# Half of w_down as seven products of block sums, with weight sums on VectorE and some low parts by DMA

## The chip, the cores and the metric

The kernel runs on one core of a Trainium2 chip. The metric is the device time of one execution in microseconds (us). The kernel before takes 1104.13 us, the median of three runs (1103.97 to 1104.59).

## The reference, cut to what matters

One layer of a decoder trunk on 256 positions of 2048 channels, in float32. A mixing part (combined projection, convolution, matrix memory, gating, output projection) is followed by the part that the change rewrites:

```python
hm = rmsnorm(x, ln_mlp_g[l]) @ w_up[l]               # (256, 2048) @ (2048, 8192)
x = x + jnp.square(jax.nn.relu(hm)) @ w_down[l]      # (256, 8192) @ (8192, 2048)
return rmsnorm(x, final_g)
```

## The kernel before, in words

TensorE multiplies in fp32r, a rounded form of float32, so every operand is cut in two: a high part (rounded) and a low part (the rest). A product of two cut operands needs three matmuls: high by high, high by low, low by high.

All weights come as pieces of 128 x 2048 floats (1 MB), loaded by SyncE in the order of use into a ring of 4 buffers (`raw`). A piece is two units of 128 x 1024. For each unit ScalarE casts the high part (`hi`, L131) and VectorE subtracts it from the raw values (`lo`, L132); each has 5 buffers. `advance(h)` is called before the matmuls of unit h: it issues loads up to 6 pieces ahead and cuts units up to 4 ahead. A scheduler sets the order on PE, ACT, DVE and SP, with the cutting of weights raised in priority; GpSimd keeps the program's order.

The MLP goes in four quarters of 2048 hidden channels. In the up half of a quarter, 16 tiles of 128 hidden channels are made, two to a PSUM pair of banks (`up`): each tile takes 16 wide matmuls of 512 columns (high weights by high and low x, L217) and 16 narrow ones of 256 columns (low weights by high x, L222). PSUM holds two such pairs, so that one fills while the other is read out: ScalarE copies one half to `u_sb` (L675), VectorE adds the other half (`u_t`, L677), takes the squared ReLU (L678), and u is cut (L679, L680). In the down half, four column blocks of 512 are made for the two halves of the 256 rows, 16 k tiles each: three matmuls of 512 columns for every k tile and row half (`dn`, L240 to L242). VectorE adds the result times the norm's factor to the residual `xr` (L694). In the last quarter the final norm follows (L698 to L718), with products by `final_g` on GpSimd (L700).

An eighth of the MLP is thus 8 up tiles, and 8 k tiles x 4 column blocks x 2 row halves x 3 = 192 matmuls of w_down.

Of the kernel before, what the change touches and what calls it, by code (L numbers as in the profile page):

```python
# [14 lines left out]
P = 128  # L15
# [8 lines left out]
DFF = 8192  # L24
NQ = 4
EPS = 1e-6
RAW_BUFS = 4
W_BUFS = 5
SPLIT_AHEAD = 4
DMA_AHEAD = 12  # L30
UNITS = 2
TAIL = 4
# [26 lines left out]
def trunk(ctx: ExitStack, tc: tile.TileContext, x, xt, w_t, w_n, w_o, w_u, w_d, gw, gm_w, cols, rows, out):  # L59
    nc = tc.nc  # L60
    const = ctx.enter_context(tc.tile_pool(name="const", bufs=1))
    big = ctx.enter_context(tc.tile_pool(name="big", bufs=1))
    wpool = ctx.enter_context(tc.tile_pool(name="wpool", bufs=W_BUFS))
    work = ctx.enter_context(tc.tile_pool(name="work", bufs=1))
    two = ctx.enter_context(tc.tile_pool(name="two", bufs=2))
    small = ctx.enter_context(tc.tile_pool(name="small", bufs=1))
    acc = ctx.enter_context(tc.tile_pool(name="acc", bufs=2, space=PSUM))
    misc = ctx.enter_context(tc.tile_pool(name="misc", bufs=4, space=PSUM))
# [7 lines left out]
    pieces = [w_n[i] for i in range(8)]  # L76
    pieces += [w_t[i] for i in range(16)]
    pieces += [w_n[i] for i in range(8, 32)]
    pieces += [w_o[i] for i in range(16)]
    for q in range(NQ):  # L80
        pieces += [w_u[q * 16 + i] for i in range(16)]
        pieces += [w_d[q * 16 + i] for i in range(16)]
    raws, his, los = {}, {}, {}
    state = {"dma": 0, "split": 0, "later": {}}
    n_units = len(pieces) * UNITS

    def load_piece():
# [9 lines left out]
        elif j < 4:  # L97
            for i in range(2):
                k = 4 * j + 2 * i
                nc.sync.dma_start(xs4[:, k:k + 2, :], xt3[:, k:k + 2, :])  # L100
                nc.sync.dma_start(raw[:, i * 1024:(i + 1) * 1024], pieces[j][:, i * 1024:(i + 1) * 1024])
        else:
# [11 lines left out]

    def split_unit():

        h = state["split"]
        state["split"] += 1
        parts = 1
        if h < 4 * UNITS:  # L120
            kn = 4 // UNITS
            for k in range(h * kn, (h + 1) * kn):
                x_prep(k)
            parts = 2 if h < P2 else 1
        raw = raws[h // UNITS][:, h % UNITS * UW:(h % UNITS + 1) * UW]
# [49 lines left out]
    cmask = const.tile([P, P], F32, name="cmask")  # L175
# [28 lines left out]
    def mm_t(pt, act, j, order=range(2 * UNITS)):  # L204
# [3 lines left out]
        for n, o in enumerate(order):  # L208
# [581 lines left out]
```

## Time and profile before

| | |
|---|---|
| median of three runs | 1104.13 us |
| the profiled execution's own time | 1103.79 us |
| its span in the profile | 1102.1 us |
| PE busy | 1089.6 us, 99% of the span |
| DVE busy | 689.6 us, 63% |
| ACT busy | 530.7 us, 48% |
| POOL busy | 57.8 us, 5% |
| granted TensorE clock | 0.998 of full speed |
| DMA | 211.05 MB, mean 191 GB/s |

PE's busy time counts matmuls whose modelled durations overlap, so that a busy PE is one that never waits, and the distance from start to start is the cost of a matmul. For DVE and ACT, too, an instruction that follows at once starts some 0.1 us before the end shown for the one ahead. Times in the rows below count from the span's start.

### The profile page before, as it was taken

What the parts mean: (1) busy time and instruction counts of PE and PEld (TensorE: products, weight loads), DVE (VectorE), ACT (ScalarE), POOL (GpSimd) and SP (SyncE); (2) the same over time, 40 slices, a digit from 0 to 9 for tenths busy, and PEclk for the clock granted to TensorE, in tenths of its full rate; (3) what the DMA queues carried; (4) which work ended last, traced back from release to release, by engine and by line L of the source; (5) the groups of instructions that cost most, each with busy time, mean ns of one, the idle gap of its engine ahead of it and who ended that gap; (6) DMA issues with size and microseconds to landing.
All of it is one profiled execution on the core that took longest, in us unless ns stands there. A gap on an engine that the chain in (4) does not pass through costs nothing.

```text
span 1102.1 us, 13677 instructions
## 1 busy us (share of the span) xinstructions
PE 1089.6 (99%) x5447; PEld 924.1 (84%) x5447; DVE 689.6 (63%) x841; ACT 530.7 (48%) x655; POOL 57.8 (5%) x70
## 2 busy tenths in 40 slices
PE   9999999999999999999999999999999999999997
PEld 7888888888888888888888888888888888888885
DVE  7788999665665556555546565555565555565553
ACT  7574755444564454443334443334444334444442
POOL 1002120040300000000000000000000000000111
PEclk9999999999999999999999999999999999999999
DMA  9645445554475555555555555555555555555531
GB/s 347 261 172 179 167 163 190 182 191 169 175 305 186 180 189 186 187 183 194 194 210 184 186 178 193 196 197 202 186 189 180 194 198 205 189 183 177 196 141 76
DMA packets 32176, 211.05 MB, mean 191 GB/s; under 512 B 3697, under 2 KB 4081, under 8 KB 7665
## 3 DMA queue, kind: packets, MB, share of 16 engines
q1 hardware_dynamic: 32112, 210.19, 54.1%
q8 instruction: 42, 0.69, 0.3%
q14 instruction: 22, 0.17, 0.0%
HBM read 208.08 MB, written 2.10 MB: 191 GB/s over the span
## 4 chain that ended last, share of the span: by engine, by line
PE 90%; DVE 5%; issue 3%; POOL 1%; ACT 1%; DMA 0%; SPq 0%; ACTq 0%; POOLq 0%; DVEq 0%
PE up L217 21%; PE up L222 11%; PE dn L242 10%; PE dn L241 10%; PE dn L240 10%; PE wo L240 3%; PE wo L242 3%; PE wo L241 3%; PE qk L217 2%; DVE lo L132 2%; DVE cvo L313 2%; PE o L240 1%; PE o L242 1%; PE o L241 1%; PE v L241 1%
## 5 line engine op out<-in xcount | busy, mean ns | idle before, releaser
L132 DVE TENSOR_TENSOR lo<-raw,hi 128x1024 fp32r<-128x1024 f32 (+1 forms) x388 | 474.6, 1226 | 340.8 <-ACT hi L131 340.6
L131 ACT CAST hi<-raw 128x1024 fp32r<-128x1024 f32 (+1 forms) x388 | 402.8, 1042 | 449.7 <-PE dn L242 188.7
L217 PE MATMUL up<-x,hi 128*128 128x512 f32 x1024 | 245.6, 391 | 0.0
L217 PEld LDWEIGHTS up<-x,hi 128*128 128x128 f32 x1024 | 188.0, 188 | 36.2
L240 PE MATMUL dn<-hi,u 128*128 128x512 f32 x480 | 186.7, 389 | 0.0
L241 PE MATMUL dn<-lo,u 128*128 128x512 f32 x480 | 186.7, 389 | 0.0
L242 PE MATMUL dn<-hi,u 128*128 128x512 f32 x480 | 186.7, 389 | 0.0
L222 PEld LDWEIGHTS up<-x,lo 128*128 128x128 f32 x1024 | 131.4, 191 | 5.1
L222 PE MATMUL up<-x,lo 128*128 128x256 f32 x1024 | 133.0, 283 | 0.0
L241 PEld LDWEIGHTS dn<-lo,u 128*128 128x128 f32 x480 | 90.1, 188 | 18.8
L240 PEld LDWEIGHTS dn<-hi,u 128*128 128x128 f32 x480 | 90.1, 188 | 18.7
L242 PEld LDWEIGHTS dn<-hi,u 128*128 128x128 f32 x480 | 90.1, 188 | 18.7
L217 PE MATMUL qk<-xg,hi 128*128 128x512 f32 x256 | 62.4, 392 | 1.0 <-DVE qk_t L413 1.0
L217 PEld LDWEIGHTS qk<-xg,hi 128*128 128x128 f32 x256 | 46.7, 188 | 10.9 <-PE qk L217 1.8
L313 DVE SCALAR_TENSOR_TENSOR cvo<-aT,colv,cvo 128x256 f32<-128x256 f32 x120 | 53.9, 498 | 0.0
L240 PE MATMUL wo<-hi,mix 128*128 128x512 f32 x128 | 50.4, 394 | 0.0
L241 PE MATMUL wo<-lo,mix 128*128 128x512 f32 x128 | 50.1, 391 | 0.0
L242 PE MATMUL wo<-hi,mix 128*128 128x512 f32 x128 | 49.9, 390 | 0.0
L700 POOL TENSOR_TENSOR xr<-xr,fgv 128x512 f32<-128x512 f32 x6 | 9.5, 1606 | 765.9 <-ACT jf L698 765.9
L679 ACT CAST u<-u_t 128x512 fp32r<-128x512 f32 x32 | 19.9, 621 | 53.0 <-DVE u_t L678 53.0
L680 DVE TENSOR_TENSOR u<-u_t,u 128x512 fp32r<-128x512 f32 x32 | 22.1, 691 | 19.3 <-ACT u L679 19.3
L222 PEld LDWEIGHTS qk<-xg,lo 128*128 128x128 f32 x256 | 32.9, 191 | 1.3
(224 smaller groups left out, 1006.5 us busy)
## 6 DMA issues: line engine op xcount, KB each, us to landing
raw<-in_w_u SPq DMA_DIRECT2D x64, 1024.0 KB, 4.7
raw<-in_w_d SPq DMA_DIRECT2D x64, 1024.0 KB, 4.7
raw<-in_w_n SPq DMA_DIRECT2D x28, 1024.0 KB, 4.7
raw<-in_w_t SPq DMA_DIRECT2D x16, 1024.0 KB, 4.7
raw<-in_w_o SPq DMA_DIRECT2D x16, 1024.0 KB, 4.8
raw<-in_w_n SPq DMA_DIRECT2D x6, 512.0 KB, 7.6
xr<-in_x SPq DMA_DIRECT2D x2, 1024.0 KB, 6.5
out<-xr SPq DMA_DIRECT2D x8, 256.0 KB, 2.6
```

What stands on the lines that cost most here:

```text
L131: nc.scalar.copy(hi[:, s], raw[:, s])
L132: nc.vector.tensor_tensor(out=lo[:, s], in0=raw[:, s], in1=hi[:, s].bitcast(F32), op=ALU.subtract)
L217: nc.tensor.matmul(pt[:, i, :], lhsT=hi[:, kk, :], rhs=act[:, k, :, :], start=(k == 0), stop=(k == NK - 1))
L222: nc.tensor.matmul(pt[:, i, 0:T], lhsT=lo[:, kk, :], rhs=act[:, k, 0, :], start=False, stop=False)
L240: nc.tensor.matmul(pt[t], lhsT=xh, rhs=hi[:, kk, :], start=(k == 0), stop=False)
L241: nc.tensor.matmul(pt[t], lhsT=xh, rhs=lo[:, kk, :], start=False, stop=False)
L242: nc.tensor.matmul(pt[t], lhsT=xl, rhs=hi[:, kk, :], start=False, stop=(k == NK - 1))
L313: nc.vector.scalar_tensor_tensor(out=o, in0=a, scalar=w, in1=o, op0=ALU.mult, op1=ALU.add)
L679: nc.scalar.copy(u[:, 2 * g:2 * g + 2, 0, :], tt)
L680: nc.vector.tensor_tensor(out=u[:, 2 * g:2 * g + 2, 1, :], in0=tt, in1=u[:, 2 * g:2 * g + 2, 0, :].bitcast(F32), op=ALU.subtract)
L700: nc.gpsimd.tensor_tensor(out=xr[:, t, cs], in0=xr[:, t, cs], in1=fgv[:, cs], op=ALU.mult)
```

## The change

Seven of the eight stages of 1024 hidden channels form columns 0 to 1023 of the down product by a 2 x 2 x 2 scheme with seven products: the blocks are two row halves, two k tiles and two column blocks of 512. Of the blocks of u (A11, A12, A21, A22) four sums are formed on GpSimd (S1 to S4, `up_out`), of the four blocks of w_down four sums on VectorE (`sum_piece`, tiles `sa` and `sb`); seven products of three matmuls each go to seven PSUM banks (`dn_a`), over four pairs of k tiles. `dn_out` puts them together into `xr`, on VectorE and GpSimd. Columns 1024 to 2047, and all of the last stage, go as before (`mm_n`, tiles `dp` and `dl`).

The up tiles of the next stage are interleaved: between the products of a pair stand two up tiles, each in the eighth bank (tag `up`, one buffer). The squared ReLU is now a square of ReLU(up) times the norm's factor, which is broadcast along the columns once by two small matmuls, so that the residual gets a plain sum.

A pair's weights are one piece with four units (512 or 1024 columns wide, with their own buffers, two of the wide and one of the narrow kind). For six of the eight up tiles of a stage the low part of the second unit is formed by a DMA on GpSimd's queue: ScalarE writes `hi`, which is `raw` rounded, and `lo`, which is minus `raw` rounded (so it costs ScalarE two operations and VectorE none), and the DMA adds `raw` to `lo`, reading the raw buffer. The raw ring has 3 buffers in place of 4, cutting goes 5 units ahead, and sums are taken 2 pieces ahead. In the query and key projections, narrow and wide matmuls alternate (`mm_t`).

```diff
--- before.py
+++ after.py
+NS = 8
+NP = 4
-RAW_BUFS = 4
+RAW_BUFS = 3
 W_BUFS = 5
-SPLIT_AHEAD = 4
-DMA_AHEAD = 12
+SPLIT_AHEAD = 5
+DMA_AHEAD = 6
+SUM_AHEAD = 2
 UNITS = 2
+ADDED = (0, 1, 3, 4, 5, 7)
...
+    for st in range(NS):
+        last = st == NS - 1
+        for g in range(0 if last else NP):
+            jdn[st, g] = stream(w_pair(st, g))
+            four.add(jdn[st, g])
+            for i in range(2):
+                sl = 2 * g + i
+                j = jup[st + 1, sl] = stream(w_u[(st + 1) * 2 * NP + sl])
+                units += [(jdn[st, g], 2 * i), (jdn[st, g], 2 * i + 1), (j, 0), (j, 1)]
+                if sl in ADDED:
+                    added.add((j, 1))
...
+    def sum_piece():
+
+        j = state["sum"]
+        state["sum"] += 1
+        if j not in four:
+            return
+        raw = raws[j]
+        s13 = ph["mlp"].tile([P, 1024], F32, tag="sum", name=f"sa{j}", bufs=2)
+        s24 = ph["mlp"].tile([P, 1024], F32, tag="sum", name=f"sb{j}", bufs=2)
+        nc.vector.tensor_tensor(out=s13.rearrange("p (a n) -> p a n", a=2),
+                                in0=raw[:, 512:1536].rearrange("p (a n) -> p a n", a=2),
+                                in1=raw[:, 0:512].rearrange("p (a n) -> p a n", a=1).broadcast_to([P, 2, 512]),
+                                op=ALU.add)
+        nc.vector.tensor_tensor(out=s24[:, 0:512], in0=s13[:, 512:1024], in1=raw[:, 512:1024], op=ALU.add)
+        nc.vector.tensor_tensor(out=s24[:, 512:1024], in0=s24[:, 0:512], in1=raw[:, 1536:2048], op=ALU.add)
+        sums[j] = (s13, s24)
...
+        pool, tag, bufs = (wpool, "", None) if j not in four else (ph["mlp"], "4", 2) if n == UW else (ph["mlp"], "5", 1)
+        hi = pool.tile([P, n], F32R, tag="hi" + tag, name=f"hi{h}", bufs=bufs)
+        lo = pool.tile([P, n], F32R, tag="lo" + tag, name=f"lo{h}", bufs=bufs)
+        his[h], los[h] = hi, lo
+        if (j, k) in added:
+            nc.scalar.copy(hi, src)
+            nc.scalar.mul(lo, src, -1.0)
+            nc.gpsimd.dma_start(out=lo, in_=src, accum_op=ALU.add)
+            return
...
+            for kk in range(kn):
+                k = o % UNITS * kn + kk
+                a = dict(lhsT=hi[:, kk, :], rhs=act[:, k, :, :])
+                b = dict(lhsT=lo[:, kk, :], rhs=act[:, k, 0, :])
+                if k < NK - 1:
+                    nc.tensor.matmul(pt[:, i, :], start=(k == 0), stop=False, **a)
+                    nc.tensor.matmul(pt[:, i, 0:T], start=False, stop=False, **b)
+                else:
+                    nc.tensor.matmul(pt[:, i, 0:T], start=False, stop=False, **b)
+                    nc.tensor.matmul(pt[:, i, :], start=False, stop=True, **a)
...
+    banks = ctx.enter_context(tc.tile_pool(name="banks", bufs=7, space=PSUM, reuse_waits="tile"))
+
+    def bank(name, tag="dn", bufs=None):
+        return banks.tile([P, 512], F32, tag=tag, name=name, bufs=bufs)
...
+    def up_out(pt, st, sl):
+
+        g, i = divmod(sl, 2)
+        if i == 0:
+            uf[st, g] = mlp.tile([P, 8, P], F32, tag="uf", name=f"uf{st}_{g}", bufs=2)
+        u = uf[st, g]
+        sb = mlp.tile([P, T], F32, tag="usb", name=f"usb{st}_{sl}")
+        nc.scalar.copy(sb, pt[:, T:2 * T])
+        q = mlp.tile([P, T], F32, tag="uq", name=f"uq{st}_{sl}", bufs=2)
+        nc.vector.tensor_tensor(out=q, in0=pt[:, 0:T], in1=sb, op=ALU.add)
+        nc.vector.scalar_tensor_tensor(out=q, in0=q, scalar=0.0, in1=rb, op0=ALU.max, op1=ALU.mult)
+        nc.scalar.activation(u[:, 0:4:3, :] if i == 0 else u[:, 1:3, :], q.rearrange("p (t n) -> p t n", t=2), AF.Square)
+        if i == 1 and st < NS - 1:
+            nc.gpsimd.tensor_tensor(out=u[:, S3:S1 + 1, :], in0=u[:, A21:A21 + 1, :].broadcast_to([P, 2, P]),
+                                    in1=u[:, A11:A22 + 1:2, :], op=ALU.subtract)
+            nc.gpsimd.tensor_tensor(out=u[:, S2, :], in0=u[:, A11, :], in1=u[:, S1, :], op=ALU.subtract)
+            nc.gpsimd.tensor_tensor(out=u[:, S4, :], in0=u[:, A12, :], in1=u[:, S2, :], op=ALU.subtract)
...
+    def split(d, u):
+        nc.scalar.copy(d[:, :, 0, :], u)
+        nc.vector.tensor_tensor(out=d[:, :, 1, :], in0=u, in1=d[:, :, 0, :].bitcast(F32), op=ALU.subtract)
+
+    def split_pair(st, g):
+        u = uf.pop((st, g))
+        ua[st, g] = mlp.tile([P, 4, 2, P], F32R, tag="ua", name=f"ua{st}_{g}", bufs=2 * NP)
+        split(ua[st, g], u[:, 0:4, :])
+        if st < NS - 1:
+            us[st, g] = mlp.tile([P, 4, 2, P], F32R, tag="us", name=f"us{st}_{g}", bufs=NP)
+            split(us[st, g], u[:, 4:8, :])
...
+            ah, al = form(st, g, a)
+            cs = slice(b * 512, (b + 1) * 512)
+            nc.tensor.matmul(acc7[a], lhsT=ah, rhs=hi[:, cs], start=(g == 0), stop=False)
+            nc.tensor.matmul(acc7[a], lhsT=ah, rhs=lo[:, cs], start=False, stop=False)
+            nc.tensor.matmul(acc7[a], lhsT=al, rhs=hi[:, cs], start=False, stop=(g == NP - 1))
...
+        nc.scalar.copy(p1, acc7[A11])
+        dve(x12, x12, acc7[S4], ALU.add)
+        dve(x11, x11, acc7[A12], ALU.add)
+        dve(x12, x12, acc7[S1], ALU.add)
+        dve(x22, x22, acc7[S1], ALU.add)
+        dve(v, p1, acc7[S2], ALU.subtract)
+        dve(w, v, acc7[S3], ALU.subtract)
+        dve(x21, x21, acc7[A22], ALU.add)
+        pool(x11, x11, p1, ALU.add)
+        pool(x12, x12, v, ALU.subtract)
+        pool(x21, x21, w, ALU.add)
+        pool(x22, x22, w, ALU.subtract)
...
+    for st in range(NS - 1):
+        acc7 = {}
+        for g in range(NP):
+            dn_a(st, g, 0, ((A11, 1), (S4, 0)), acc7)
+            dn_a(st, g, 1, ((A12, 0),), acc7)
+            up_tile(st + 1, 2 * g)
+            dn_a(st, g, 2, ((S1, 1), (S3, 0)), acc7)
+            dn_a(st, g, 3, ((S2, 0), (A22, 1)), acc7)
+            if g == NP - 1:
+                dn_out(st, acc7)
+            up_tile(st + 1, 2 * g + 1)
+        for c in (2, 3):
+            pt = [bank(f"dp{st}_{c}{t}") for t in range(2)]
+            mm_n(pt, act_n(st), jpl[st, c], nk=2 * NP)
```

ScalarE around an up tile's end, before. `hi` is a high part, `u_sb` the copy out of PSUM, `u1` the cut of u; the number behind a name tells units and buffers apart, and in brackets stand the engines or queues waited for.

```order
L131 CAST hi226_5278<-raw113_5092 128x1024 [waits DMAHW0_49,PE_49,Activation_49]
L131 CAST hi227_5298<-raw113_5092 128x1024 [waits PE_49,Activation_49]
L131 CAST hi228_5328<-raw114_5142 128x1024 [waits DMAHW1_49,PE_49,Activation_49]
L675 COPY u_sb17_5318<-up17_5233 128x512
L131 CAST hi229_5344<-raw114_5142 128x1024 [waits PE_49,Activation_49]
L679 CAST u1_4588<-u_t17_5320 128x2x256 [waits DVE_49]
```

And now, at the end of the first up tile of a stage (`up3_0`; `sa` is a weight sum, `uf` the values of u, `usb` the copy, and raw109 holds the next-but-two piece of w_up).

```order
L205 CAST hi233_5412<-raw107_5218 128x512 [waits DMAHW3_49,PE_49]
L205 CAST hi234_5424<-raw108_5257 128x1024 [waits DMAHW4_49]
L205 CAST hi235_5439<-raw108_5257 128x1024 [waits PE_49]
L205 CAST hi238_5507<-raw109_5296 128x1024 [waits DMAHW5_49,PE_49]
L785 COPY usb3_0_5406<-up3_0_5356 128x256
L205 CAST hi232_5385<-raw107_5218 128x1024 [waits DMAHW2_49,PE_49]
L205 CAST hi236_5459<-sa107_5359 128x1024 [waits DVE_49,PE_49]
L789 ACTIVATE uf3_0_5405<-uq3_0_5408 128x2x128 [waits DVE_49]
```

In both, a cast stands directly ahead of the copy that frees the tile's bank; now this cast waits for a load (DMAHW5) as well as for PE.

TensorE from one up tile to the next, before: the tile in the other pair of banks follows at once.

```order
L217 MATMUL up15_5049<-x2_2597,hi215_5022 128x512 [waits Activation_49]
L217 MATMUL up15_5049<-x2_2597,hi215_5022 128x512 x7
L217 MATMUL up16_5141<-x2_2597,hi216_5052 128x512 [waits DVE_49]
L217 MATMUL up16_5141<-x2_2597,hi216_5052 128x512 x7
L222 MATMUL up16_5141<-x2_2597,lo216_5053 128x256 x8
```

And now, the last three of the thirteen product matmuls that stand between tiles `up3_0` and `up3_1`, and the whole of `up3_1`.

```order
L832 MATMUL dn2_2_5432<-lo229_5336,ua2_0_4704 128x512
L833 MATMUL dn2_2_5432<-hi229_5336,ua2_0_4704 128x512
L831 MATMUL dn2_0_5340<-hi232_5385,ua2_1_4859 128x512 [waits Activation_49]
L765 MATMUL up3_1_5436<-x2_2607,hi230_5348 128x512 [waits DVE_49]
L765 MATMUL up3_1_5436<-x2_2607,hi230_5348 128x512 x7
L769 MATMUL up3_1_5436<-x2_2607,lo230_5349 128x256 x8
L769 MATMUL up3_1_5436<-x2_2607,lo231_5365 128x256 [waits DMASW5_49]
L769 MATMUL up3_1_5436<-x2_2607,lo231_5365 128x256 x7
L765 MATMUL up3_1_5436<-x2_2607,hi231_5364 128x512 x8
```

The tile's first matmul waits for VectorE's add out of the only `up` bank, and its second low part for a DMA of GpSimd's queue.

GpSimd before: between the mixing part and the last quarter's norm nothing stands in its queue.

```order
L192 TENSOR_TENSOR lnc_2556<-lnr_2554,nhalf_106 128x2 [waits DVE_49]
L608 TENSOR_TENSOR og_2240<-og_2240,numx_791 128x512 [waits Activation_49] x2
L700 TENSOR_TENSOR xr_2594<-xr_2594,fgv_3290 128x512 [waits DMAHW2_49,DMAHW6_49,Activation_49,Pool_49]
L700 TENSOR_TENSOR xr_2594<-xr_2594,fgv_3290 128x512 [waits DMAHW3_49,PE_49,Activation_49]
L700 TENSOR_TENSOR xr_2594<-xr_2594,fgv_3290 128x512 [waits Activation_49]
```

And now, from the putting together of stage 1 to the adding DMAs at the start of stage 2 (`p1`, `v`, `w` are sums of products).

```order
L843 TENSOR_TENSOR xr_2604<-xr_2604,p11_5109 128x512 [waits DVE_49]
L843 TENSOR_TENSOR xr_2604<-xr_2604,v1_5110 128x512 [waits DVE_49]
L843 TENSOR_TENSOR xr_2604<-xr_2604,w1_5111 128x512 [waits DVE_49]
L843 TENSOR_TENSOR xr_2604<-xr_2604,w1_5111 128x512
L791 TENSOR_TENSOR uf2_3_5082<-uf2_3_5082 128x256 [waits Activation_49]
L793 TENSOR_TENSOR uf2_3_5082<-uf2_3_5082 128x128 [waits Pool_49]
L794 TENSOR_TENSOR uf2_3_5082<-uf2_3_5082 128x128 [waits Pool_49]
L200 DMA lo227_5299<-raw105_5125 128x1024 [waits DMASW3_49,DMAHW0_49,DVE_49,PE_49]
L200 DMA lo231_5365<-raw106_5184 128x1024 [waits DMASW0_49,DMAHW1_49,DVE_49,Activation_49]
L791 TENSOR_TENSOR uf3_0_5405<-uf3_0_5405 128x256 [waits Activation_49]
```

The two DMAs stand behind the sums of u of the stage's last pair, and ahead of those of the next.

## Rows read from the trace of the kernel before

**Rows 1.** The page, part 1 and the first line of part 4.

```profile
PE 1089.6 (99%) x5447; PEld 924.1 (84%) x5447; DVE 689.6 (63%) x841; ACT 530.7 (48%) x655; POOL 57.8 (5%) x70
...
PE 90%; DVE 5%; issue 3%; POOL 1%; ACT 1%; DMA 0%; SPq 0%; ACTq 0%; POOLq 0%; DVEq 0%
```

**Rows 2.** The longest waits of PE: who waited for whom, us, times, longest.

```profile
PE warm L163 <- DVE warm L159: 1.1, 1, 1.1
PE qk L217 <- DVE qk_t L413: 1.0, 2, 0.7
```

**Rows 3.** Busy time by stretch, the MLP without its last block.

```profile
core 0: us, PE busy (x) PEld busy (x) DVE busy (x) ACT busy (x) POOL busy (x), PEclk, DMA share, GB/s
...
390.00:1007.00 617.00, 617.00 (x3203) 530.84 (x3203) 350.46 (x348) 270.81 (x294) 0.00 (x0) 1.00 0.55 191
```

**Rows 4.** PE in order of time: start, us, operation; one quarter's down and up halves.

```profile
478.42 0.39 PE L240 MATMUL dn<-hi,u 128*128 128x512 f32 x1
478.64 0.39 PE L241 MATMUL dn<-lo,u 128*128 128x512 f32 x1
...
565.46 0.84 PE L217 MATMUL up<-x,hi 128*128 128x512 f32 x3
...
654.52 0.39 PE L240 MATMUL dn<-hi,u 128*128 128x512 f32 x1
```

**Rows 5.** DVE by line and shape: busy us, mean ns of one, idle before.

```profile
L132 DVE TENSOR_TENSOR lo<-raw,hi 128x1024 fp32r<-128x1024 f32 x380 | 469.4, 1238 | 338.8 <-ACT hi L131 338.7
L680 DVE TENSOR_TENSOR u<-u_t,u 128x512 fp32r<-128x512 f32 x32 | 22.1, 691 | 19.3 <-ACT u L679 19.3
L424 DVE SCALAR_TENSOR_TENSOR qk_c<-qk_z,colv,qk_c 128x256 f32<-128x256 f32 x48 | 20.9, 478 | 5.9 <-ACT qk_c L421 5.7
L355 DVE TENSOR_TENSOR scr<-gps,scr 36x256 f32<-36x256 f32 x1 | 0.4, 409 | 0.0
```

**Rows 6.** ACT by line and shape, columns as in Rows 5.

```profile
L131 ACT CAST hi<-raw 128x1024 fp32r<-128x1024 f32 x380 | 398.2, 1051 | 447.8 <-PE dn L242 188.7 <-PE up L217 135.5 <-PE wo L242 36.6
L473 ACT COPY numx<-num 128x258 f32<-128x258 f32 x8 | 2.7, 375 | 0.5 <-PE num L472 0.5
```

**Rows 7.** ACT and DVE in order of time at an up half's end.

```profile
478.66 1.05 ACT L131 CAST hi<-raw 128x1024 fp32r<-128x1024 f32 x1 [2.69 <-PE up L217]
479.62 0.57 ACT L675 COPY u_sb<-up 128x512 f32<-128x512 f32 x1
...
479.75 1.23 DVE L132 TENSOR_TENSOR lo<-raw,hi 128x1024 fp32r<-128x1024 f32 x1 [2.52 <-ACT hi L131]
480.89 0.68 DVE L677 TENSOR_TENSOR u_t<-up,u_sb 128x512 f32<-128x512 f32 x1
```

**Rows 8.** DVE and POOL in order of time, 1030 to 1036 us.

```profile
1030.02 1.22 DVE L132 TENSOR_TENSOR lo<-raw,hi 128x1024 fp32r<-128x1024 f32 x1
1032.55 2.17 DVE L132 TENSOR_TENSOR lo<-raw,hi 128x1024 fp32r<-128x1024 f32 x1 [1.31 <-ACT hi L131]
...
1030.50 3.14 POOL L700 TENSOR_TENSOR xr<-xr,fgv 128x512 f32<-128x512 f32 x2 [728.75 <-ACT jf L698]
```

**Rows 9.** POOL by line and shape, columns as in Rows 5.

```profile
L571 POOL TENSOR_TENSOR sq<-sq 128x512 f32<-128x512 f32 x1 | 1.3, 1296 | 5.8 <-ACT sq L570 5.8
L554 POOL TENSOR_TENSOR csum<-cvo 128x256 f32<-128x256 f32 x1 | 0.7, 737 | 0.0
```

**Rows 10.** DMA issues: KB each, median us to landing.

```profile
raw<-in_w_u SPq DMA_DIRECT2D x64, 1024.0 KB, 4.7
raw<-in_w_n SPq DMA_DIRECT2D x6, 512.0 KB, 7.6
gng<-in_rows SPq DMA_DIRECT2D x1, 512.0 KB, 4.2
```

**Rows 11.** GB/s in 40 slices of 498 to 520 us (0.55 us each).

```profile
GB/s 432 45 0 0 0 209 89 402 372 447 387 0 0 0 0 134 179 402 447 447 313 15 0 0 0 238 89 343 477 432 328 15 0 0 0 223 209 343 432 447
```

More of the change, by code (lines that the diff above doesn't have):

```diff
@@ L101, in load_piece @@
                 nc.sync.dma_start(raw[:, i * 1024:(i + 1) * 1024], pieces[j][:, i * 1024:(i + 1) * 1024])
+        elif j in four:
+            for i in range(2):
+                nc.sync.dma_start(raw[:, i * 1024:(i + 1) * 1024], pieces[j][i])
         else:
@@ L118, in split_unit @@
         state["split"] += 1
+        j, k = units[h]
         parts = 1
@@ L264, in trunk @@
     pt = acc_tile("cg")
-    mm_n(pt, xg, 0)
+    mm_n(pt, halves(xg), 0)
     for o_ in (0, 4):
@@ new lines, in trunk, with up_units, wide, narrow @@
+    uf, ua, us = {}, {}, {}
+    def up_units(pt, j, k):
+        kn = NK // UNITS
+        h = index[j, k]
+        hi = his.pop(h).rearrange("p (k n) -> p k n", k=kn)
+        lo = los.pop(h).rearrange("p (k n) -> p k n", k=kn)
+        def wide():
+            for kk in range(kn):
+                kt = k * kn + kk
+                nc.tensor.matmul(pt, lhsT=hi[:, kk, :], rhs=x2[:, kt, :, :], start=(kt == 0), stop=(kt == NK - 1))
+        def narrow():
+            for kk in range(kn):
+                nc.tensor.matmul(pt[:, 0:T], lhsT=lo[:, kk, :], rhs=x2[:, k * kn + kk, 0, :], start=False, stop=False)
+        if k == 0:
+            wide()
+            narrow()
+        else:
+            narrow()
+            wide()
@@ new lines, in trunk @@
+    for k in range(UNITS):
+        for sl in range(2):
+            j = jup[0, sl]
+            if k == 0:
+                us["pt", sl] = bank(f"up0_{sl}")
+            advance(index[jup[0, 0], 0] + 2 * k + sl)
+            up_units(us["pt", sl], j, k)
+    rps = bank("rps")
+    for t in range(2):
+        dg = mlp.tile([P, P], F32, tag="usb", name=f"r_dg{t}")
+        nc.vector.tensor_scalar(out=dg, in0=ident, scalar1=r2[:, t:t + 1], scalar2=None, op0=ALU.mult)
+        nc.tensor.matmul(rps[:, t * P:(t + 1) * P], lhsT=ones, rhs=dg, start=True, stop=True)
@@ new lines, in trunk, with norm_part @@
+                nc.vector.tensor_tensor(out=xr[:, t, cs], in0=pt[t], in1=xr[:, t, cs], op=ALU.add)
+    st = NS - 1
+    fgv = keep.tile([P, D], F32, tag="A", name="fgv")
+    nc.sync.dma_start(fgv, rows[0:1, R_FG:R_FG + D].broadcast_to([P, D]))
+    def norm_part(c, t):
+        cs = slice(c * 512, (c + 1) * 512)
+        jk = mlp.tile([P, 512], F32, tag="p1", name=f"jf{c}{t}")
+        nc.scalar.activation(jk, xr[:, t, cs], AF.Square, accum_out=st3[:, t, c:c + 1])
+        if c < 3:
+            nc.gpsimd.tensor_tensor(out=xr[:, t, cs], in0=xr[:, t, cs], in1=fgv[:, cs], op=ALU.mult)
```

278 lines of the change are left out of this document (154 added, 124 removed).

## Prediction

> **What bounds the kernel now.** I read the page's shares first: TensorE is busy for 99% of the span, and 90% of the chain that ended last runs over it [rows 1]. Then its waits: the longest two are 1.1 and 1.0 us [rows 2], so nothing is to be won by taking waits away. By stretches, from 390 to 1007 us TensorE is busy for 617 of 617 us at the full clock, VectorE for 351 (57%), ScalarE for 271 (44%), and the DMA engines are 55% busy [rows 3]. The kernel's time is its number of matmuls times their pitch; the other engines have slack, and the change spends it.
>
> The pitch comes from the starts in order of time [rows 4]: a quarter's down half begins at 478.42, its up half at 565.46, the next down half at 654.52. The first is 384 matmuls of 512 columns: 87.04 / 384 = 0.2267 us each. The second is 16 up tiles: 89.06 / 16 = 5.566 us each. Of VectorE's and ScalarE's operations I take durations [rows 5, 6], and where they follow at once the distance of the starts, about 0.1 less: a low part of 1024 costs 1.14 us (479.75 to 480.89), a cast 0.96 (478.66 to 479.62) [rows 7].
>
> **What is removed.** A stage's w_down takes 192 matmuls now. The half that is rewritten had 96 and gets 7 products x 4 pairs x 3 = 84. That is 12 fewer in each of seven stages, 84 x 0.2267 = **-19.0 us**. A stage is then 8 x 5.566 + (84 + 96) x 0.2267 = 85.3 us long, where it was 88.1. That wide and narrow matmuls alternate in the query and key projections I cost at nothing: the same matmuls stand there, and TensorE goes from one kind to the other within each up tile now without a wait [rows 2, 4]. The norm's tail keeps its operations.
>
> **The single bank for up tiles.** Before, the next tile goes to another pair of banks. Now its first matmul waits until ScalarE's copy and VectorE's add have emptied the only bank; product matmuls fill the time between. The order gives their number ahead of a stage's tiles 1 to 7: 13, 8, 12, 9, 12, 13, 13, or 2.95, 1.81, 2.72, 2.04, 2.72, 2.95 and 2.95 us. Undisturbed, emptying takes: start of the copy 0.24 after the tile's end (478.42 to 478.66 for the first operation of ScalarE [rows 4, 7]), the copy 0.375 by a 258-column one [rows 6], the add 0.41 by a 256-column one [rows 5], together 1.03: hidden everywhere. But casts and low parts have raised priority, and behind tiles 0, 5 and 6 the order puts a cast directly ahead of the copy and a low part ahead of the add. The trace has just this: cast at 478.66, copy 479.62, low part 479.75, add 480.89 [rows 7]. With 0.41 for the add the bank is free at 481.30, 2.88 us after 478.42, against 2.95. That is a tie, and I charge 0.2 us to each of the three. In the windows of 1.81 and 2.04 a low part that has just begun makes 1.03 + 1.14 = 2.17, late by 0.36 or 0.13; not every time, so 0.1 each. Sum 0.8 a stage, x 7 = **+5.6**. Bounds: 0, and one low part's 1.14 at each of the seven tiles, 8.0 a stage, 56 us.
>
> **The adding DMAs and three raw buffers.** No row shows a DMA that adds. From a 512 KB load's 4.2 us at the least to 7.6 at the most, where 1 MB lands in 4.7 [rows 10]: of the 4.7 about 2.4 us are movement (in the slices, four or five of 0.55 us at some 400 GB/s, then a gap [rows 11]), so 2.3 are fixed. A DMA that adds reads two times 512 KB, each 1.2 us of movement: 2.3 + 2.4 = 4.7, my estimate. As lower bound 3.5 (2.3 and one 512 KB movement); upper 7.6.
>
> What waits for it: the tightest place is a stage's start. There the order has the DMA for the second tile's low part (the one with DMASW5) behind ScalarE's multiplication, which comes about 1.7 us ahead of the stage's first product by the order of casts. When it has landed, raw's buffer may be loaded again (4.7 us), and the cast of that load stands directly ahead of the copy that frees the bank of the stage's first tile. So the cast can begin at D - 1.7 + 4.7 = D + 3.0; that tile ends after 9 products and itself, 2.04 + 5.57 = 7.6, and 0.24 later ScalarE would take the cast. Hidden up to D = 4.8. At 4.7 it is a tie again: 0.1 in six stages, **+0.6**. TensorE's own wait for that low part has more: tiles 0 and 1 and the products between lie ahead. A later adding DMA of the same stage stands on GpSimd behind the sums of u; it starts about 14.5 us into the stage and is needed at 21.2, so it is hidden up to D = 6.7.
>
> By the Trainium skill ("DMA: Bandwidth & Descriptors", section "Anatomy of one DMA — SWDGE (gpsimd) path") a DMA of GpSimd's queue takes 2.0 us and its bytes at 436 GB/s. By "Collectives: The Full Stack" of the Trainium skill (section "The bandwidth ceiling: the fold count and why AG ≠ RS ≠ AR") an add needs two source reads and goes at about half the rate. Both together would be 2.0 + 2.4 = 4.4 us, an estimate by which this term falls to 0; no trace here shows such a DMA.
>
> **VectorE.** For each stage of 85.3 us: 30 low parts of 1024 (six of 36 are gone to the DMAs, twelve belong to the pairs) x 1.14 = 34.2; four weight sums of the same width 4.6; 31 operations of 512 (eight sums, four low parts, eight of u, seven of the putting together, four residuals) x 0.60, from 0.69 less 0.1 = 18.6; eight adds and eight ReLU operations of 256, (0.41 + 0.48 - 0.18) x 8 = 5.7 [rows 5, 7]. Sum 63.1, or 74%. On top comes GpSimd: a low part that runs beside one of GpSimd's operations with two inputs takes 2.17 in place of 1.22 us [rows 8]. GpSimd gets, a stage, four times an operation of 256 (0.74) and two of 128 (0.46 each, estimated from 0.74 and 1.30), and four of 512 (1.30) [rows 9], 11.8 us. If VectorE stood for all of that, it has 75 of 85.3 us: tight, and still not the bound.
>
> The Trainium skill ("SBUF — State Buffer", section "Who interferes with whom") says that a VectorE instruction with two SBUF inputs and a GpSimd instruction that reads SBUF exclude each other wholly. By that rule all of the 11.8 us count; the trace agrees, with 2.17 beside 1.22 us, so that the 75 is taken as it stands.
>
> **The rest.** Start of the MLP with three raw buffers, two small matmuls that broadcast the norm's factor, and the hand-overs of banks between products and plain blocks: 1.5 us, **+1.5**, from about one exposed low part (1.14) and one add (0.41); bounds 0 and 6 (a 1 MB load, 4.7, exposed once, and one low part). ScalarE has, a stage, 36 casts and six multiplications of 0.96, and some 12 us of smaller ones: 52 of 85.3, no bound.
>
> **Sum.** -19.0 + 5.6 + 0.6 + 1.5 = -11.3. The profiled execution took 1103.79 us (1102.1 of it span); 1092.5, and the median of the runs lies 0.34 above that one: **1093 us**.
>
> **Rivals.**
> First, everything is hidden: neither bank nor DMA costs anything. For it: free emptying takes 1.03 us against 1.8 to 2.95, and VectorE and ScalarE have slack. Against it: raised priority of casts, as in rows 7. -19.0 + 1.5 = -17.5, **1087 us**. Chance 0.20.
>
> Second, VectorE becomes the bound. 75 us of work lie in a fixed order with waits for ScalarE, for PE and for GpSimd; 338.8 us of its idle time now lie ahead of low parts, behind casts [rows 5], about 0.9 for each. With 2 us of idle time in each of a stage's eight tiles it takes 75 + 16 = 91, 5.7 over, x 7 = 40: 1103.8 - 19.0 + 40 = **1125 us**. It decides from (85.3 - 75) / 8 = 1.3 us of idle time a tile. Against it: low parts are cut five units ahead. Chance 0.10.
>
> Third, and mainly on the slower side, the adding DMA lands late, through the raw buffers. At D = 7.6 the reload holds ScalarE's queue by 7.6 - 4.8 = 2.8 us and the later low part is late by 7.6 - 6.7 = 0.9, in six stages: 22.2. With 5.6 and 1.5: -19.0 + 29.3 = +10.3, **1114 us**. It makes the kernel slower from D = 6.75 on: at 6.7 the 1.9 x 6 = 11.4 us nearly use up the 11.9 that are left of the gain, and beyond it grows by 12 us for each us of D. For it: 512 KB loads of 7.6 us exist; a raw ring of three gives little play. Against it: those pieces are halves of one load that queue behind each other, and the other 512 KB one took 4.2. Chance 0.15.
>
> **How the numbers follow.** The forecast has 0.55; its own range is 1088 to 1099 (bank term between 0.2 and 1.7 a stage). A measurement here tells some 0.2%, 2.2 us, from no change. Faster: the forecast's 0.52, the first rival's 0.20 and a little of the third, 0.73; slower: 0.10 and most of the third, and the forecast's tail, 0.19; same 0.08. The range leaves out the second rival and the outer part of the others: 1085 to 1114.
>
> **What would show it.** TensorE's matmuls of 512 columns at the same 0.227 us pitch, and 84 fewer. In TensorE's waits, a group of up tiles behind VectorE's add, of 0.1 to 0.3 us in about five of eight tiles: the bank term. ScalarE's casts behind raw loads at the stages' starts: the raw term; and low parts of up tiles behind GpSimd's DMA queue, which should hardly be there. Adding DMAs that land in 4 to 5 us. VectorE at 80 to 90% of a stage, with low parts of 2 us beside GpSimd's sums. The prediction is wrong if VectorE stands above 95% in a stage, or if adding DMAs take over 6.5 us, or if TensorE's waits come to under 2 or over 15 us in all.

## The result, and the profile after

The changed kernel takes 1192.85 us (median of four runs, 1187.45 to 1196.28) against 1104.05 of the kernel before: 1.0799 times as long, 95% interval 1.0756 to 1.0842. The prediction was 1093 us, 1085 to 1114, faster with a chance of 0.73. It was wrong on the side as well as in size. Of its own signs of being wrong one showed: TensorE's waits of 68 us, where over 15 was its limit.

First the page after, its shares and the first line of its chain, then TensorE's waits (who waited for whom, us, times, longest); they answer to [rows 1, 2]:

```profile
PE 1111.0 (93%) x5367; PEld 931.5 (78%) x5367; DVE 833.9 (70%) x1086; ACT 649.8 (54%) x884; POOL 210.7 (18%) x225
...
PE 59%; DMA 17%; issue 7%; ACT 7%; POOL 5%; DVE 4%; SPq 0%; POOLq 0%; ACTq 0%; DVEq 0%
```

```profile
PE up L765 <- DVE uq L787: 48.6, 16, 5.4
PE dn L831 <- ACT hi L205: 19.8, 8, 3.9
```

TensorE had two waits of 1 us before; now two groups make up 68.4 us, and DMAs have 17% of the chain that had 0%. By stage (columns as in [rows 3]; seven stages with products, each from its first product on):

```profile
434.00:537.00 103.00, 91.81 (x439) 77.44 (x438) 73.57 (x88) 59.55 (x80) 26.87 (x28) 0.93 0.61 197
537.00:639.00 102.00, 91.45 (x437) 76.56 (x436) 68.94 (x82) 54.16 (x71) 21.22 (x23) 0.93 0.60 195
639.00:742.00 103.00, 91.37 (x439) 76.15 (x438) 69.32 (x83) 54.29 (x72) 21.77 (x23) 0.95 0.60 194
742.00:844.50 102.50, 91.68 (x438) 77.09 (x437) 69.64 (x82) 54.71 (x71) 21.71 (x23) 0.93 0.62 197
844.50:943.80 99.30, 90.24 (x437) 75.80 (x436) 69.08 (x82) 54.40 (x71) 22.37 (x22) 0.95 0.62 200
943.80:1045.00 101.20, 91.26 (x437) 76.51 (x436) 69.12 (x82) 54.29 (x71) 21.50 (x23) 0.95 0.61 198
1045.00:1140.00 95.00, 89.75 (x437) 75.07 (x437) 59.73 (x73) 47.97 (x62) 10.07 (x9) 0.96 0.68 219
```

They take 706 us where the prediction's 85.33 a stage make 597.3: all of the loss is here. What lies ahead and behind takes 1192.7 - 706 = 486.7 us; before, with seven stages of 88.05 taken off, it is 485.7. The 108.7 us divide in two. 68.4 are TensorE's waits. The rest, 40.3 us, is time in which TensorE is busy, 637.6 us of these stages by the rows above where 597.3 would do; and the granted clock accounts for about that much: one minus the shares 0.93 to 0.96, times each stage's length, summed, is 40 us. The clock falls after a wait; three stretches around one of them (same columns):

```profile
676.30:683.87 7.57, 2.18 (x11) 1.49 (x9) 2.81 (x4) 4.67 (x6) 0.00 (x0) 0.98 0.77 300
683.87:687.50 3.63, 3.63 (x11) 2.92 (x12) 3.63 (x5) 1.41 (x3) 2.54 (x3) 0.57 0.01 2
691.00:700.00 9.00, 9.00 (x49) 7.77 (x48) 5.19 (x7) 5.74 (x8) 0.00 (x0) 1.00 0.82 305
```

TensorE is busy for 2.18 of 7.57 us and waits for the rest; then it works without a pause at 0.57, mostly its 1.2 GHz level, for 3.6 us; a few us later it has 2.4 GHz again. A wait of 5.4 us so costs 1.6 us more (3.63 x 0.43), after other waits up to 2.7 (an up tile of 32 matmuls, 5.34 us from its first to its last start, takes 8.09 at 479.83). The prediction had no such term.

Where a wait comes from, the chain shows (start, us, what), in the third of these stages, which begins at 639.17:

```profile
637.12 1.07 ACT lo L199
...
638.48 5.58 DMA lo<-raw
...
644.20 6.45 DMA raw<-in_w_u
...
650.73 0.07 ACT hi L205
...
651.68 0.37 ACT usb L785
652.05 0.95 ACT hi L205
...
653.05 0.79 PE dn L831
653.84 3.19 PE up L765 x8
...
667.47 1.05 ACT lo L199
...
668.83 5.95 DMA lo<-raw
...
675.29 6.84 DMA raw<-in_w_d
...
682.25 1.23 DVE sa L167
683.48 0.35 DVE uq L787
```

ScalarE writes minus raw, the DMA adds raw, only then the same raw buffer is loaded again, only then ScalarE can cast the new piece (650.73). Behind that cast ScalarE's queue has the copy that empties the bank of the stage's first tile (651.68), and behind the copy the cast of a high part (652.05). What TensorE waits for here is this high part, for 3.4 us: a product ahead of the second tile needs it (L831; in six of the seven stages the first long wait is of this kind). The bank was no earlier: VectorE's add ended at 653.74, and the tile started at 653.79. Behind the fourth tile it is the same chain, with a weight sum on VectorE (`sa`) between the load and the add, and there TensorE waits for the bank. A third stall, of 2.6 to 2.7 us ahead of the last tile in six of the seven stages, has no raw load in the end of its chain:

```profile
711.86 0.68 DVE xr L840
712.53 1.14 DVE lo L206
713.67 0.35 DVE uq L787
...
714.06 2.31 PE up L765 x5
```

There the operations that put the products together (L840) and a low part stand ahead of the add. So does the cut of u ahead of them, and it is slow (VectorE and GpSimd in order of time):

```profile
709.75 2.19 DVE L808 TENSOR_TENSOR us<-uf,us 128x512 fp32r<-128x512 f32 x1 [1.55 <-ACT us L807]
...
709.77 1.60 POOL L843 TENSOR_TENSOR xr<-xr,p 128x512 f32<-128x512 f32 x1
```

It takes 2.19 us beside GpSimd's addition of a product to `xr`, 2.13 to 2.19 at this place in six stages, where this operation has a median of 0.68: about 1.5 of the 2.66 us of this wait.

### The profile page after: what moved, and what is told of

Read it like the earlier page. It is cut to its first block, busy times and chain, and to the rows that moved or that the text cites. A ratio compares the mean times of both kernels' runs of the same rounds, so it can differ in the third digit from the quotient of the medians.

```text
span 1192.7 us, 14235 instructions
## 1 busy us (share of the span) xinstructions
PE 1111.0 (93%) x5367; PEld 931.5 (78%) x5367; DVE 833.9 (70%) x1086; ACT 649.8 (54%) x884; POOL 210.7 (18%) x225
## 4 chain that ended last, share of the span: by engine, by line
PE 59%; DMA 17%; issue 7%; ACT 7%; POOL 5%; DVE 4%; SPq 0%; POOLq 0%; ACTq 0%; DVEq 0%
PE up L765 11%; DMA lo<-raw 8%; DMA raw<-in_w_u 6%; PE qk L293 5%; PE up L769 4%; DMA raw<-in_w_d 4%; ACT hi L205 3%; PE dp L315 3%; PE dp L314 3%; PE dp L313 3%; PE wo L313 2%; PE wo L315 2%; PE wo L314 2%; PE qk L294 2%; POOL uf L791 2%
## 5 line engine op out<-in xcount | busy, mean ns | idle before, releaser
L206 DVE TENSOR_TENSOR lo<-raw,hi 128x1024 fp32r<-128x1024 f32 (+1 forms) x346 | 418.0, 1215 | 233.0 <-ACT hi L205 226.4
L205 ACT CAST hi<-raw 128x1024 fp32r<-128x1024 f32 (+1 forms) x346 | 344.0, 1004 | 325.3 <-DMA raw<-in_w_u 91.3
L765 PE MATMUL up<-x,hi 128*128 128x512 f32 x1024 | 280.6, 420 | 48.6 <-DVE uq L787 48.6
L313 PE MATMUL dp<-hi,ua 128*128 128x512 f32 x224 | 87.1, 389 | 0.0
L315 PE MATMUL dp<-hi,ua 128*128 128x512 f32 x224 | 87.1, 389 | 0.0
L314 PE MATMUL dp<-lo,ua 128*128 128x512 f32 x224 | 87.1, 389 | 0.0
L294 PE MATMUL qk<-xg,lo 128*128 128x256 f32 x240 | 67.4, 281 | 0.0
L831 PE MATMUL dn<-hi,ua 128*128 128x512 f32 x84 | 34.9, 415 | 19.8 <-ACT hi L205 19.8
L198 ACT CAST hi<-raw 128x1024 fp32r<-128x1024 f32 x42 | 43.8, 1042 | 12.3 <-PE up L765 12.3
L199 ACT ACTIVATE lo<-raw 128x1024 fp32r<-128x1024 f32 x42 | 44.4, 1057 | 10.3 <-PE dp L314 8.1
L313 PEld LDWEIGHTS dp<-hi,ua 128*128 128x128 f32 x224 | 42.0, 188 | 8.8
```

Source lines behind the costliest of these rows:

```text
L199: nc.scalar.mul(lo, src, -1.0)
L205: nc.scalar.copy(hi[:, s], src[:, s])
L206: nc.vector.tensor_tensor(out=lo[:, s], in0=src[:, s], in1=hi[:, s].bitcast(F32), op=ALU.subtract)
L294: nc.tensor.matmul(pt[:, i, 0:T], start=False, stop=False, **b)
L313: nc.tensor.matmul(pt[t], lhsT=xh, rhs=hi[:, kk, :], start=(k == 0), stop=False)
L314: nc.tensor.matmul(pt[t], lhsT=xh, rhs=lo[:, kk, :], start=False, stop=False)
```

## The experiments

All times are medians, all ratios are against the kernel before, run on the same chip.

**No adding DMA (noadd).**

```diff
-ADDED = (0, 1, 3, 4, 5, 7)
+ADDED = ()
```

> The changed kernel with no adding DMA: all low parts on VectorE again, raw ring still 3, one bank still. Theory H (an adding DMA and the reload of the same raw buffer stand in series, and ScalarE and VectorE have work that waits for that load ahead of the emptying of the bank): TensorE's waits fall from 68 us to under 15, its granted clock goes back to 0.99 or more, and the 40 us of half-speed matmuls go: 1192.85 - 55 - 40 = about 1095 us (1088 to 1105). Theory R (three raw buffers are too few by themselves, whoever frees them): half of the waits stay, 1130 to 1170. Theory V (VectorE, which gets 6 x 1.14 = 6.9 us more in each stage, is the bound): VectorE over 90% of a stage and 1110 to 1130.

Measured: 1130.4 us, ratio 1.0245 (1.0228 to 1.0262). TensorE's waits for bank and high parts fall from 68.4 to 22 us, the clock goes to 0.992. So the adding DMAs cost 62 us, but theory H explains only that much: 45 us above 1085 (the time with stages of 85.3) stay. Up to 20 of these may be an accident: the scheduler put 48 products between two tiles of the first stage, which took 108.5 us; later ones take 87.5 to 90. The time lies at the edge of what theories R and V had given; VectorE has 75 of some 88.5 us of a later stage, 85%, under the 90 of theory V.

**A fourth raw buffer (ring4).**

```diff
-RAW_BUFS = 3
-W_BUFS = 5
+RAW_BUFS = 4
+W_BUFS = 4
```

> The adding DMAs stay; the raw ring has 4 buffers, paid for by 4 in place of 5 buffers for high and low parts. Theory H: a reload has a whole piece more of play (some 5 us), which covers the three stalls of 2.8 to 5.5 us of a stage: 1100 to 1125 us. If the adding DMAs harm in another way (slower loads beside them, low parts that come late themselves, GpSimd beside VectorE), it stays above 1160. Four buffers for the parts may cost some of it back: the mixing part, which ends at 388 us now, tells how much.

1128.3 us, 1.0226 (1.0211 to 1.0241), 3 us above the range of theory H and far under 1160. Nearly the same gain with the adding DMAs in place: most of what they cost comes from holding one buffer of three. The edit also leaves four buffers for the parts in place of five, so that it does not tell the ring's share alone. Here, too, some 43 us are left; TensorE's largest wait is for the add (22.9 us).

**Another order (order).**

```diff
-SPLIT_AHEAD = 5
-HP = 200
+SPLIT_AHEAD = 3
+HP = 0
```

> The same work, DMAs and buffers in another order: cutting without raised priority and 3 units ahead in place of 5. At a stage's start the copy that empties the bank then stands ahead of the cast that waits for the latest load (one of the two late loads there is still ahead of it), and at the fourth tile the add stands ahead of the weight sum that waits for its load. Theory H with the queues' order as the harmful half: the stall of about 5.4 us at the fourth tile goes with its half-speed matmuls, and 1 to 1.5 us at the stage's start: 7 x (5.4 + 2.5 + 1.4) = 65, about 1130 us (1115 to 1150). If what comes late is needed at once whatever the order: the stalls move to other matmuls and it stays within 1180 to 1200.

1203.71 us, 1.091 (1.0892 to 1.0927): slower; the first expectation fell, and the second was passed by 4 us. Its waits of TensorE:

```profile
PE up L765 <- DVE uq L787: 37.1, 22, 3.6
PE up L769 <- DMA lo<-raw: 24.3, 7, 5.1
PE dn L831 <- ACT hi L205: 6.7, 6, 1.8
PE dn L832 <- DVE lo L206: 5.7, 6, 1.0
```

They are 74 us in place of 68, and 24 of them stand directly at a low part that the DMA has not landed. So the late weights are needed soon after whatever the order. That three buffers alone make them late is not shown by this run: the edit also cuts 3 units ahead in place of 5, which by itself starts every adding DMA later.

**The DMA without the add (plain).**

```diff
-            nc.gpsimd.dma_start(out=lo, in_=src, accum_op=ALU.add)
+            nc.gpsimd.dma_start(out=lo, in_=src.bitcast(F32R))
```

> The DMA of GpSimd's queue only copies raw to the low part and adds nothing, so these low parts are not the right ones; order, buffers and waits are as in the changed kernel. It moves 512 KB in place of reading two times 512 KB. Theory H: it lands in 3.3 to 4.4 us in place of 5.1 to 6, and each of a stage's three stalls, which holds one such DMA in its chain, is some 1.5 us shorter: 7 x 3 x 1.5 = 31 us less, and a part of the half-speed time: 1140 to 1165 us. Theory R, or a harm that is not in the DMA's duration: within 10 us of 1193.

1152.13 us, 1.0433 (1.0404 to 1.0461), 40.7 less. DMA issues (KB, median us to landing; columns as in [rows 10]), first of the changed kernel, then of this one:

```profile
raw<-in_w_u SPq DMA_DIRECT2D x64, 1024.0 KB, 4.9
...
lo<-raw POOLq DMA_DIRECT2D x42, 512.0 KB, 5.1
```

```profile
lo<-raw POOLq DMA_DIRECT2D x42, 512.0 KB, 3.1
```

And TensorE's two large waits, to be set beside 48.6 and 19.8:

```profile
PE up L765 <- DVE uq L787: 32.8, 19, 3.6
PE dn L831 <- ACT hi L205: 8.0, 4, 3.0
```

They are 27.6 us less, 3.9 a stage for 2.0 us off each DMA: the stalls at the stage's start and behind the fourth tile shrink, each by some 2 us, nearly one for one, and the third one, ahead of the last tile, only from 2.65 to 2.33. The other 13 of the 40.7 us go with the clock (0.979 of full speed over the run, where it was 0.965). Even at 3.1 us the DMAs cost 22 us against the run without them (1152.1 - 1130.4).

**Two banks for up tiles, adding DMAs kept (bank2).** The product of A22 is added up in the bank of A11 (the first and last matmuls of the two are marked to fit).

```diff
-    banks = ctx.enter_context(tc.tile_pool(name="banks", bufs=7, space=PSUM, reuse_waits="tile"))
+    banks = ctx.enter_context(tc.tile_pool(name="banks", bufs=6, space=PSUM, reuse_waits="tile"))
...
-        pt = bank(f"up{st}_{sl}", tag, 1 if tag == "up" else None)
+        pt = bank(f"up{st}_{sl}", tag, 2 if tag == "up" else None)
...
-                acc7[a] = bank(f"dn{st}_{a}")
+                acc7[a] = acc7[A11] if a == A22 else bank(f"dn{st}_{a}")
...
```

> The changed kernel with its adding DMAs and ring of 3, but two banks for up tiles: the product of A22 is added up in the bank of A11, so that the columns of those two products are not the right ones; the number of matmuls is the same, TensorE's order nearly so (9 or 12 products between tiles). Theory B (late loads cost time only because they hold up the emptying of the one bank): 1090 to 1115 us. Theory T (the loads are late for TensorE's own operands a few us later, as the run in another order made likely, and the ring turns too slowly): the waits move from the bank to high and low parts, 1150 to 1190.

1175.1 us, 1.0644 (1.0628 to 1.066). Theory T: the second bank only lets TensorE run on to the next thing that is late.

```profile
PE up L769 <- DMA lo<-raw: 55.1, 18, 6.2
PE dn L832 <- DVE lo L206: 9.8, 13, 1.7
```

**TensorE in the program's order (noadd_pe).**

```diff
-ADDED = (0, 1, 3, 4, 5, 7)
+ADDED = ()
-IN_ORDER = [ET.Pool]
+IN_ORDER = [ET.Pool, ET.PE]
```

> No adding DMA, ring 3, one bank, and TensorE held to the program's order (always 9 or 12 products between up tiles), since without adding DMAs the scheduler had put 48 products in one place of the first stage, which then took 108 us in place of the 88.5 of later ones. Stages of about 88.5: 1130 - 20 = 1110 us (1104 to 1118). This is the base for the next two.

1136.19 us, 1.0288 (1.0273 to 1.0304): a miss. The accident of the first stage is gone from the order, not from the time (100.8 us, with a wait of 7.0 ahead of the second tile), and stages stay at 90 to 92. About 5 us are lost ahead of the first product (439.4 us from the start, 434.3 in the run noadd_bank2; TensorE waits 4.2 us for transposed inputs in this order). What is left is the single bank, as the next run shows. How emptying goes here, ScalarE and then VectorE in order of time; the tile ended at 730.00, and TensorE starts the next at 732.91:

```profile
730.20 1.05 ACT L205 CAST hi<-raw 128x1024 fp32r<-128x1024 f32 x1 [2.62 <-PE up L765]
731.16 0.36 ACT L785 COPY usb<-up 128x256 f32<-128x256 f32 x1
...
731.29 1.23 DVE L206 TENSOR_TENSOR lo<-raw,hi 128x1024 fp32r<-128x1024 f32 x1 [0.68 <-ACT hi L205]
732.43 0.42 DVE L787 TENSOR_TENSOR uq<-up,usb 128x256 f32<-128x256 f32 x1
```

The cast waits for TensorE (2.62 us): the end of the tile frees the high part's buffer that it writes. So it becomes ready at the moment the copy does, has the higher priority, and the low part behind it comes ahead of the add. In the order of this run a cast and a low part stand there behind six of a stage's eight tiles, in most stages. It costs little where the window is 2.72 us, as here, and a wait of 0.7 where it is 2.04. After the first stage the longest wait of a stage, 1.9 to 2.2 us in most, stands ahead of the last tile, where an operation of the putting together comes in between as well.

**Two banks without adding DMAs (noadd_bank2).** The edit of bank2 and `ADDED = ()`.

> The kernel without adding DMAs, TensorE's order as in the run before, and two banks for up tiles (products A11 and A22 share one, their columns are not the right ones). What it gains against that run is the price of the single bank, which the prediction put at 0.8 us a stage, 5.6 in all. If the single bank is what is left of the loss: stages of 85.5 to 86.5, 1087 to 1097 us. If VectorE's work is the bound: 1105 or more, with VectorE at the same share of a stage.

1085.44 us, 0.9829 (0.9813 to 0.9846). The first and the last of the seven stages:

```profile
434.30:519.70 85.40, 85.40 (x438) 73.17 (x438) 78.97 (x94) 50.69 (x71) 23.73 (x21) 1.00 0.54 192
...
946.30:1031.70 85.40, 85.40 (x438) 73.17 (x438) 65.25 (x79) 44.84 (x58) 6.28 (x4) 1.00 0.56 201
```

TensorE waits nowhere in them, with VectorE busy for 92% of the first of them and a ring of three; the time is 1.6 us under the range expected. Against the run before, with the same sequence of tiles and products on TensorE, the single bank costs 1136.2 - 5.0 - 1085.4 = 46 us. Theory V is out, and so is theory R, for the kernel without adding DMAs.

**A fourth raw buffer without adding DMAs (noadd_ring4).** The run noadd_pe with the edit of ring4.

> No adding DMA, one bank, TensorE in the same order, raw ring 4 in place of 3 (and 4 buffers for the parts in place of 5). Theory R (three raw buffers cost time by themselves): 8 us or more below the run with three. Otherwise the same within 4 us: then the ring was too short only for a buffer that is also held by an adding DMA.

1162.25 us, 1.0525 (1.0509 to 1.0541): 26 us slower than with three, neither of the two. The edit also takes a buffer from the high and low parts, and with that more casts wait for a tile's end (95, where it was 76): TensorE's wait for the add is 47.6 us, 41 times, where it was 28.8. On the ring it says nothing; noadd_bank2 does, with three buffers and no wait.

**Fourth buffer and second bank, adding DMAs kept (ring4_bank2).** Both edits.

> The adding DMAs stay, raw ring 4 (and 4 buffers for parts), two banks for up tiles (A11 and A22 share one, their columns are not the right ones). If the adding DMAs cost time only by holding one of three raw buffers for some 5 us, a fourth buffer and the second bank together leave nothing: stages of 85.3 to 86.5, 1085 to 1094 us. If low parts that land late cost time by themselves: TensorE's waits for GpSimd's DMA queue stay (55 us with ring 3), 1110 or more.

1099.93 us, 0.9956 (0.9939 to 0.9973): 75 us below bank2, between the two expectations. TensorE's waits for GpSimd's DMA queue fall from 55.1 to 6.9 us. So with two banks the DMAs cost mainly by holding a buffer of three; the 14.5 us that are left above the run noadd_bank2 are theirs or those of the four buffers for the parts, which these runs do not part.

**Emptying first (first).** The run noadd_pe, and:

```diff
+UP_HP = 500
...
-        nc.scalar.copy(sb, pt[:, T:2 * T])
...
-        nc.vector.tensor_tensor(out=q, in0=pt[:, 0:T], in1=sb, op=ALU.add)
+        with tc.high_priority(UP_HP):
+            nc.scalar.copy(sb, pt[:, T:2 * T])
+            nc.vector.tensor_tensor(out=q, in0=pt[:, 0:T], in1=sb, op=ALU.add)
```

> No adding DMA, ring 3, one bank, TensorE in the program's order as in the run noadd_pe (1136 us); the only edit is that the copy and the add that empty the bank have a higher priority than the cutting of weights. After six of a stage's tiles the copy then stands ahead of the cast that waits for the same tile's end (for the high part's buffer which that end sets free), where it stood behind it. If that cast and the low part behind it are what makes emptying take 2.9 us in place of 1.03: TensorE's waits for the add fall from 28.8 us to 5 to 12, and with the half-speed stretches behind them the time to 1092 to 1112 us. If VectorE's backlog holds the add anyway: within 8 us of 1136.

1106.09 us, 1.0025 (1.001 to 1.004), 30 less. TensorE's wait:

```profile
PE up L766 <- DVE uq L789: 12.0, 15, 1.6
```

12.0 us in place of 28.8, and a granted clock of 1.00 in all seven stages, where noadd_pe had 0.97 in the first. What stood in front of the copy and the add, the cast and the low part above all, was about two thirds of the bank's price, 30 of 46 us. The edit puts the copy and the add ahead of whatever else is in the two queues too, so that it does not price the cast alone.

**A version that keeps the gain (six).** No adding DMA; the twelve matmuls of the product of A12 stand behind a stage's last up tile, with their blocks of w_down loaded once more, so that six banks hold products and two hold up tiles.

```diff
...
+            odd = [w_down(0, 2 * st + i).rearrange("p (a b n) -> p a b n", a=2, b=2)[:, :, 1, :] for i in range(2)]
+            jod[st] = stream(odd)
...
-            dn_a(st, g, 1, ((A12, 0),), acc7)
...
```

> A version that computes the reference: no adding DMA, and two banks for up tiles, because the product of A12 is not kept open across the up tiles: its blocks of w_down are loaded once more (1 MB a stage) and its 12 matmuls stand behind the last up tile. Matmuls as in the changed kernel. If the single bank and the adding DMAs are all that was lost: every stage at 85.3 us, 1084 to 1090 us, ratio to the kernel before 0.982 to 0.987. If the 17th load of a stage is too much for the ring of 3: waits for high parts at raw loads, 1095 or more.

1089.68 us, 0.9868 (0.9853 to 0.9883): 1.3% under the kernel before, and faster than the changed one. The first line of its page, and TensorE's largest wait:

```profile
PE 1075.0 (99%) x5367; PEld 908.9 (83%) x5367; DVE 883.5 (81%) x1114; ACT 606.2 (56%) x828; POOL 189.1 (17%) x183
```

```profile
PE dn L839 <- DVE lo L213: 2.3, 3, 1.0
```

Its stages take 87.6 us at first and 85.3 from the fifth on; the four above 85.3 lose 5 us in all, about what it lies above the run noadd_bank2 (4.2).

## Why the prediction was wrong, step by step

**The matmuls removed: right.** 85.3 us a stage was forecast; with both causes of waits away each of seven stages takes 85.33 us, and the kernel is 18.7 us faster, against 19.0 forecast. The query and key order and the rest of the program (+1.5 forecast) came out within about 1 us.

**The single bank: mis-sized, by a factor of eight without adding DMAs.** Forecast 5.6 us; 46 in the run noadd_pe. The prediction took 1.03 us for an undisturbed emptying and let a cast and a low part stand in front only where the order has them adjacent, at three of seven tiles, as a tie. In the order of noadd_pe, which is not the changed kernel's, they stand there at most tiles: 2.9 us, also where the window is 2.04. The run named first puts copy and add ahead of them and gets 30 of the 46 us back. In the changed kernel itself (tiles of a stage counted from 0, as in the prediction) the tie held where it was read from the order: behind tile 5 the waits are 0 to 1.0 us, and behind tiles 1, 2 and 4 there are none. What failed there, the adding DMAs apart, is tile 6. Behind it the prediction charged 0.2 us; TensorE waits 2.6 to 2.7 in six of seven stages, because VectorE's queue ahead of the add, with the putting together of products and a cut of u slowed beside GpSimd, was not priced. The slowing was counted in VectorE's total only, not in what stands in front of the add.

**The adding DMAs: the step that cost most, the third rival's mechanism at a duration at which it should not have decided.** Forecast 0.6 us; measured 62 with one bank, 90 with two (1175.1 against 1085.4). The duration was nearly right, 5.1 us against 4.7. What failed is the chain D + 3.0: by it the late cast can begin 7.7 us after the stage's start, just ahead of the 7.8 at which ScalarE would take it. In the trace it begins 11.56 after it (650.73 less 639.17). Of the 3.9 between, about 1.0 is the multiplication, which ended 0.98 ahead of the stage's start where 1.7 was counted and was followed by 0.29 to the issue; 0.9 is the DMA (5.58); 1.75 is the load, 6.45 where 4.7 was taken [rows 10]: the median rose to 4.9 only, but the two loads behind the adding DMAs of this stage's start, which run beside each other, take 6.5 and 7.0; the rest is hand-over. And the chain was worked out at one place and for one victim: the cast of a high part stands behind it too, and a product waits for that; and behind the fourth tile the chain stands again, with VectorE's weight sum in it. So the break-even of 6.75 us for D was far too high: at a median of 3.1 us (the run plain) the DMAs already cost 22 us, where the prediction had 11.9 of the gain left.

**The clock: a term that was missing.** About 40 us of the changed kernel's loss are matmuls at the lower level behind waits. The kernel before never waits in the MLP [rows 3], so that its rows could not show it.

**VectorE as the bound: rightly put low.** It has 69 us of a stage now, between the 63 and the 75 that were forecast without and with GpSimd, and in the run noadd_bank2 79 of the first stage's 85.4 us without a wait of TensorE. Low parts by DMA relieved an engine that was not the limit.

What stays open: that GpSimd's addition slows the cut of u ahead of the last tile is read from the overlap in time, and no run tested it by itself; the run noadd_ring4 was inconclusive on the ring, since four buffers for the parts alone may have made it slower; and how the 108.7 us of the changed kernel divide between bank and DMA is not a sum, as both share their chains: taking away the DMAs alone gives 62, the second bank alone 18, both 107.

## What to carry to other kernels

When a buffer is freed by the end of a piece of work, look at what else that end releases on the same engine: what has the higher priority goes first. A step that holds a buffer of a ring longer is priced by the whole loop (hold, reload, first use and whatever stands in that queue behind the first use), at every place of the period, with transfer times of the kernel as it will be. And where TensorE has never waited, a new wait can cost more than its length, since the clock may fall behind it: here 40 us beside 68 us of waits, of which most were 2 us and longer. In the run named first, with 15 waits of up to 1.6 us, the clock stayed at 1.00 in every stage.

## What the runs showed of the hardware

A DMA that adds 512 KB from one SBUF tile to another lands in 5.1 us, and one that only copies them in 3.1. In a view of 636 to 646 us, where two adding DMAs run beside each other, the DMA engines are busy for most of the time and move far less than loads do alone (1.05 MB for the two DMAs, so that each is counted with 512 KB):

```profile
DMA  0000000589996999988799989989929479989989
GB/s 0 0 0 0 0 0 33 98 164 262 246 180 131 229 262 197 180 147 148 147 229 246 180 164 197 262 164 164 197 33 459 131 295 426 492 328 459 426 360 492
```

Up to 644 us it is some 190 GB/s, behind it, with loads alone, 300 to 490. 
Beside each other, VectorE and GpSimd slow each other as in [rows 8], and by the means GpSimd pays more. Its operations by line and shape (columns as in [rows 9]):

```profile
L791 POOL TENSOR_TENSOR uf<-uf 128x256 f32<-128x256 f32 x28 | 30.4, 1086 | 472.8 <-ACT uf L789 465.4 <-DMA raw<-in_w_d 7.4
L794 POOL TENSOR_TENSOR uf<-uf 128x128 f32<-128x128 f32 x28 | 25.5, 911 | 2.2
```

256 columns take 1.09 us in place of 0.74, 128 columns 0.91 in place of the 0.46 estimated, while a low part of 1024 has a mean of 1.255 in place of 1.238. But VectorE pays too where the two meet: the cut of u (`us`, L808) has a mean of 1.00 us with a median of 0.68 and a longest of 2.19, and the long ones stand in the queue ahead of the last tile's add. In the run noadd_bank2 its mean is 0.68.
